# The inputs of a state-space convolution in a two-block kernel: four of its matmuls with whole fp32 weights

## The chip, the cores and the metric

The kernel runs on one core of a Trainium2 chip. A core has five engines, each with its own instruction order: TensorE (PE in the profile; its weight loads are shown apart as PEld), VectorE (DVE), ScalarE (ACT), GpSimd (POOL) and SyncE (SP), from which most transfers (DMAs) are issued. The metric is the device time of one execution in microseconds (us); lower is better.

## The reference

Two blocks run one after the other on 256 tokens of width 1024. The first is two layers of pooling, sparse attention and a feed-forward part. The second, which the change concerns, is a block with a state-space branch (SSD), a dilated attention branch and a feed-forward part, all in fp32. Cut to what matters here:

```python
def second_block(x, w_in, ...):
    u = h @ w_in
    z, xbc, dt_f_raw, dt_b_raw, q, k, v, gate_logits = jnp.split(u, ...)
    y_ssd = ssd_branch(z, xbc, dt_f_raw, dt_b_raw, conv_w, conv_b, ...) @ w_proj_ssd
    y_att = attention_branch(q, k, v) @ w_proj_attn
    gates = jax.nn.sigmoid(gate_logits + b_gate).reshape(bsz, s, N_BRANCHES, D_MODEL)
    mix = (gates[:, :, 0] * y_ssd + gates[:, :, 1] * y_att) @ w_out
    ...

def ssd_branch(z, xbc, ...):
    xbc = jax.nn.silu(centred_depthwise_conv(xbc, conv_w, conv_b))     # 5 taps
    xs, bm, cm = jnp.split(xbc, [D_INNER, D_INNER + SSD_GROUPS * D_STATE], axis=-1)
    ...
    y = (y_f + y_b + d_skip[:, None] * xh).reshape(...) * jax.nn.silu(z)
    # then a norm over each of the 4 groups
```

`w_in` has 1024 rows. The product `h @ w_in` is made in pieces of 512 columns; of `xbc` these are x0, x1, x2, x3 (the 2048 columns of `xs`, one piece for each of the 4 groups), B and C.

## The kernel before

*Weights.* All weights stream from HBM in chunks of 128 x 1024 fp32 (512 KB). `Weights.load` (line 129) issues a chunk's DMA on SP into a tile `wst` (5 buffers), and splits it in two: ScalarE copies it to `wh` in the type fp32r (line 140), VectorE subtracts this from `wst` and writes the rest, `wl` (line 141). `wh` and `wl` have 9 buffers each. Chunks are loaded in the order of the products, three ahead in block 2, at most four at once. `W.next()` hands out the next chunk.

*Products.* The activations are split in the same way, `hh` and `hl`. A product is three matmuls into the same PSUM bank: rest by whole, whole by rest, whole by whole. All matmuls are written by the helper `mm` (line 89), so all have line 89 in the profile and are told apart by their tiles. There are three forms. `Gemm.fm` makes the result with the channels on partitions: for each k of 128 rows and each of four column blocks, the weights are the stationary 128x128 block and 256 tokens stream (x0 to x3, B, C); records are `acc<-hh,wl 128x256`, `acc<-hl,wh`, `acc<-hh,wh`. `Gemm.tm` makes it with the tokens on partitions (q, k, v, z), streaming 512 weight columns: `acc<-wh,hl 128x512` and so on.

*Order.* In block 2 the products follow the list `order2`: v0 qk0 qk1 qk2 v1 B C x0 x1 z0 x2 z1 x3 z2 z3 g2 g3 pa g0 g1 ps. Each piece has four chunks (`x`: two k each, eight products of 128x256 a chunk). Between the products the other work of the block is issued, by generators that advance with each k: dilated attention beside B, C, x0 and x1; the state-space work of group g once xg and zg are there. The order of the instructions within each engine follows from it at build time by the scheduler of the language; on the chip each engine works its own list in that order and waits at its head.

*What follows an x.* `conv(name, c0)` (line 1316) evacuates the PSUM banks of x: ScalarE applies the middle tap and the bias (`cv<-acc,par`, line 1327), VectorE adds the other four taps (line 1330, four for each of four channel blocks, 16 in all), ScalarE makes a tanh (`page<-cv`, line 1331) and VectorE the product (line 1332). From the pages of B and C TensorE makes two products for each group (`tr<-page`, 128x256), which VectorE takes up as `cbu`, `cbl`, `cbo` (lines 1396 to 1398), and from an x page transposes (`tr<-cst,page`), which VectorE takes up as `xo` (line 1410). All of them write the one PSUM bank `tr`. ScalarE and VectorE further build decay matrices `R` and `G` (lines 1431 to 1446), with which TensorE makes `pv<-xt,R`.

*Where the activations come from.* At the end of layer 1, `done1(t)` calls `to_fm` for each half t of the tokens: TensorE transposes the residual into PSUM, ScalarE copies it to `hh` and VectorE subtracts to `hl`.

Of the kernel before, what the change touches and what calls it, by code (L numbers as in the profile page):

```python
# [17 lines left out]
S = 256  # L18
# [43 lines left out]
def tile_two_blocks(ctx: ExitStack, tc: tile.TileContext, I, out, stop=None, dbg=None):  # L62
# [59 lines left out]
    class Weights:  # L122


        def __init__(self):
            self.specs, self.ready, self.extra, self.rate, self.due = deque(), deque(), deque(), 0.0, 0.0
            self.live, self.used, self.depth, self.cap = 0, False, 0, NW

        def load(self, srcs, kc, n):
            st = wp.tile([128, SZ], FT, name="wst", bufs=NST)  # L130
            sv = st[:, :kc * n].rearrange("p (k n) -> p k n", k=kc)
            at = 0
            for src in srcs:
                w = src.shape[-1]
                nc.sync.dma_start(sv[:, :, at:at + w], src)
                at += w
            assert at == n
            h = wp.tile([128, SZ], FR, name="wh", tag="wh", bufs=NW)
            l = wp.tile([128, SZ], FR, name="wl", tag="wl", bufs=NW)
            A.activation(h[:, :kc * n], st[:, :kc * n], AF.Copy)  # L140
            V.tensor_tensor(l[:, :kc * n], st[:, :kc * n], h[:, :kc * n], op=OP.subtract)  # L141
            self.ready.append((h[:, :kc * n].rearrange("p (k n) -> p k n", k=kc),
                               l[:, :kc * n].rearrange("p (k n) -> p k n", k=kc)))
            self.due += self.rate
            while self.due >= 1.0 and self.extra:
                self.due -= 1.0
                self.step()
# [50 lines left out]
    class Gemm:  # L198


        def __init__(self, w, cols):
            self.n = sum(b - a for a, b in cols)
            self.K = w.shape[1]
            self.kc = min(self.K, SZ // self.n)
            for k0 in range(0, self.K, self.kc):
                kn = min(self.kc, self.K - k0)
                W.specs.append(([w[:, k0:k0 + kn, a:b] for a, b in cols], kn, self.n))

        def chunks(self):
            return [(k0, min(self.kc, self.K - k0)) for k0 in range(0, self.K, self.kc)]  # L210
# [19 lines left out]
        def fm(self, act, evac, tag="acc"):  # L230

            nct = self.n // 128
            banks = [bank(tag) for _ in range((nct + 1) // 2)]
            for k0, kn in self.chunks():
                h, l = W.next()
                for k in range(kn):
                    ah, al = act(k0 + k)
                    for c in range(nct):
                        o = banks[c // 2][:, (c % 2) * 256:(c % 2) * 256 + 256]
                        wh, wl = h[:, k, c * 128:(c + 1) * 128], l[:, k, c * 128:(c + 1) * 128]  # L240
                        mm(o, wl, ah, k0 + k == 0 and c % 2 == 0)
                        mm(o, wh, al, False)
                        mm(o, wh, ah, False, k0 + k == self.K - 1)
                    tick()
                    yield
            for b, p in enumerate(banks):
                evac(b, p)
# [204 lines left out]
    def new_h():  # L452
        return (xp.tile([128, 8, S], FR, name="hh", bufs=1), xp.tile([128, 8, S], FR, name="hl", bufs=1))

    def to_fm(t, xn, hi, lo, sc=None, sh=None):

        for kb in range(2):
            b = bank(("tr", "pv")[kb])
            for k in range(4):
                T.transpose(b[:, k * 128:(k + 1) * 128], xn[kb][:, k * 128:(k + 1) * 128], ident)  # L460
            src = b.rearrange("p (a b) -> p a b", a=4)
            if sc is not None:
                hf = t2([128, 4, 128], "hf")
                for k in range(4):
                    kk = kb * 4 + k
                    if kb:
                        A.activation(hf[:, k], src[:, k], AF.Identity, bias=sh[:, kk:kk + 1], scale=sc[:, kk:kk + 1])
                    else:
                        V.tensor_scalar(hf[:, k], src[:, k], sc[:, kk:kk + 1], sh[:, kk:kk + 1], op0=OP.mult, op1=OP.add)
                src = hf  # L470
            ks, tsl = slice(kb * 4, kb * 4 + 4), slice(t * 128, t * 128 + 128)
            split(hi[:, ks, tsl], lo[:, ks, tsl], src, A)


    lay = []
# [17 lines left out]
    for n in ORDER2 + ["o"]:  # L493
# [4 lines left out]
        elif n == "pa":  # L498
            g2[n] = Gemm(kt_view(I["w_proj_attn_2"]), [(0, D)])
        elif n == "ps":  # L500
            g2[n] = Gemm(kt_view(I["w_proj_ssd_2"]), [(0, D)])
        elif n == "o":
            g2[n] = Gemm(kt_view(I["w_out_2"]), [(0, D)])
        else:
            c = X0 + CONV2[n] * 128 if n in CONV2 else {"q": Q0, "z": Z0, "g": G0}[n[0]] + int(n[-1]) * 512
            g2[n] = Gemm(wi, [(c, c + 512)])
    ff2 = FeedForward(I["w_up_2"], I["w_down_2"])


# [609 lines left out]
    xn0 = [rms(t) for t in range(2)]  # L1119
    W.rate = TU["r0"]  # L1120
    W.extra.extend(mod_part(*m, TU["modp"]) for m in MODS["mix", 0])
    h1, h2_ = [], []

    def between0(c):
        if c == 4:
# [16 lines left out]
    def done1(t):  # L1142
        if not h2_:
            h2_.extend(new_h())
        to_fm(t, [xs[t][:, :512], xs[t][:, 512:]], *h2_)

    hybrid_layer(1, h1, None, done1)
    if stop == "l1":
# [167 lines left out]
    def conv(name, c0):  # L1316
# [14 lines left out]
            A.activation(fl(th), fl(cv), AF.Tanh, scale=0.5)  # L1331
            V.scalar_tensor_tensor(fl(th), fl(th), 1.0, fl(cv), op0=OP.add, op1=OP.mult)

        yield from g2[name].fm(aF, ev)
        cvo[name] = o[0]
        plan.got.add(name)

# [423 lines left out]
```

## Time and profile before

| | |
|---|---|
| time, three runs | 1280.6, 1282.55, 1288.57 us (median 1282.55) |
| profiled execution | 1284.53 us, of it 1282.4 us span |
| mean granted clock of TensorE | 0.967 |
| busy: TensorE, weight load | 1179.8 us (92%), 1037.6 us (81%) |
| busy: VectorE, ScalarE, GpSimd | 895.9 us (70%), 642.4 us (50%), 237.0 us (18%) |
| HBM read | 246.03 MB, 193 GB/s over the span |

The busy times are of the whole span. Times in the rows below count from the span's start. Block 2 begins at about 703 us; x0 begins at 787.15, x1 at 809.22, z0 at 825.97, x2 at 846.95, z1 at 861.67, x3 at 880.80, z2 at 896.98 and z3 at 921.33. A row of the timeline groups equal instructions that follow one another: its start, its length, the engine, the line, the operation, the tiles and their count. Matmuls overlap in the pipe, so that their cost is read from start to start. A wait is the time in which an engine had an instruction at its head that could not start, put down to the one that released it.

### The profile page before, as it was taken

Reading aid. Unit: us, or ns where it says so; the run is one execution under the profiler, and the core shown is the slowest. Engines: PE = TensorE matmul, PEld = TensorE weight load, DVE = VectorE, ACT = ScalarE, POOL = GpSimd, SP = SyncE. Lnnn points to the kernel's source line nnn. Section 1 sums busy time; section 2 is a strip of 40 time slices with the busy share of each in tenths; the row PEclk is TensorE's granted clock in tenths of the full one; section 3 lists DMA queues with packets and bytes.
Section 4 is the critical chain, followed back from the end, with each engine's and each line's share of the span. In section 5 each row is a group of like instructions: output and inputs, shape, how many; then the busy total and the mean of one; then the engine's idle time right before and its main releaser. Section 6 shows DMA issues by size and latency. Waiting matters only on the chain.

```text
span 1282.4 us, 19159 instructions
## 1 busy us (share of the span) xinstructions
PE 1179.8 (92%) x7188; PEld 1037.6 (81%) x7188; DVE 895.9 (70%) x1446; ACT 642.4 (50%) x1070; POOL 237.0 (18%) x233
## 2 busy tenths in 40 slices
PE   4878898999898899999999999988898899999997
PEld 3656776899787788789998999977688888799896
DVE  5777798887758768764545738799999557754544
ACT  4346355444535554744543545485675434544440
POOL 3553322112315101210100000011112001210101
PEclk9788889999999999999999999989899899999999
DMA  7855667889878534566663663564466753666640
GB/s 268 284 174 180 230 214 230 292 297 330 289 218 266 189 99 119 190 207 192 181 193 101 216 200 102 195 174 139 135 191 189 258 151 98 226 210 188 183 145 33
DMA packets 101780, 249.18 MB, mean 194 GB/s; under 512 B 9780, under 2 KB 15028, under 8 KB 101688
## 3 DMA queue, kind: packets, MB, share of 16 engines
q1 hardware_dynamic: 100904, 247.12, 60.6%
q8 instruction: 56, 0.92, 0.3%
q10 hardware_dynamic: 784, 0.85, 0.2%
q14 instruction: 36, 0.29, 0.1%
HBM read 246.03 MB, written 1.11 MB: 193 GB/s over the span
## 4 chain that ended last, share of the span: by engine, by line
PE 38%; issue 10%; DVE 8%; ACT 1%; POOL 1%; DMA 0%; DVEq 0%; POOLq 0%; ACTq 0%
PE acc L89 23%; PE st L89 12%; DVE wl L141 2%; DVE R L1444 1%; DVE cv L1330 1%; PE pv L89 1%; DVE G L1433 1%; DVE R L1446 1%; ACT wh L140 1%; POOL yss L119 0%; DVE ytmp L1465 0%; DMA wst<-in_w_up_dram 0%; PE tr L89 0%; POOL fr L380 0%; DVE yg L1477 0%
## 5 line engine op out<-in xcount | busy, mean ns | idle before, releaser
L141 DVE TENSOR_TENSOR wl<-wst,wh 128x1024 fp32r<-128x1024 f32 (+3 forms) x340 | 418.6, 1244 | 164.7 <-ACT wh L140 163.7
L140 ACT ACTIVATE wh<-wst 128x1024 fp32r<-128x1024 f32 (+3 forms) x340 | 352.1, 1048 | 314.2 <-PE acc L89 98.1
L89 PE MATMUL st<-hh,wh 128*128 128x256 f32 x576 | 163.0, 283 | 0.0
L89 PE MATMUL st<-hl,wh 128*128 128x256 f32 x576 | 163.0, 283 | 0.0
L89 PE MATMUL st<-hh,wl 128*128 128x256 f32 x576 | 163.0, 283 | 0.0
L89 PE MATMUL acc<-wh,frl 128*128 128x512 f32 x384 | 151.8, 395 | 2.4 <-DVE frl L381 2.3
L89 PE MATMUL acc<-wl,frh 128*128 128x512 f32 x384 | 150.6, 392 | 0.0
L89 PE MATMUL acc<-wh,frh 128*128 128x512 f32 x384 | 150.3, 391 | 0.0
L380 POOL TENSOR_TENSOR fr<-fr 128x512 f32<-128x512 f32 x48 | 64.7, 1349 | 384.7 <-ACT frh L379 376.4
L89 PE MATMUL acc<-hh,wl 128*128 128x256 f32 x416 | 122.1, 294 | 1.4 <-DVE wl L141 1.4
L89 PE MATMUL acc<-hl,wh 128*128 128x256 f32 x416 | 119.0, 286 | 0.0
L89 PE MATMUL acc<-hh,wh 128*128 128x256 f32 x416 | 118.7, 285 | 0.0
L89 PEld LDWEIGHTS st<-hh,wl 128*128 128x128 f32 x576 | 110.5, 192 | 0.7
L89 PEld LDWEIGHTS st<-hl,wh 128*128 128x128 f32 x576 | 110.5, 192 | 0.7
L89 PEld LDWEIGHTS st<-hh,wh 128*128 128x128 f32 x576 | 110.5, 192 | 0.0
L89 PE MATMUL acc<-wl,hh 128*128 128x512 f32 (+3 forms) x224 | 90.6, 405 | 13.1 <-DVE wl L141 13.1
L89 PE MATMUL acc<-wh,hl 128*128 128x512 f32 (+3 forms) x224 | 90.2, 413 | 12.4 <-ACT wh L140 9.9
L548 DVE SCALAR_TENSOR_TENSOR macc<-wst,cact,macc 128x1024 f32<-128x1024 f32 x70 | 91.7, 1311 | 7.5 <-DMA wst<-in_w_mod_dram 3.9
L89 PE MATMUL acc<-wh,hh 128*128 128x512 f32 (+3 forms) x224 | 90.6, 405 | 0.0
L89 PEld LDWEIGHTS acc<-wh,frl 128*128 128x128 f32 x384 | 72.6, 189 | 19.6 <-DVE frl L381 5.4
L89 PEld LDWEIGHTS acc<-wh,frh 128*128 128x128 f32 x384 | 72.5, 189 | 15.5
L89 PEld LDWEIGHTS acc<-wl,frh 128*128 128x128 f32 x384 | 72.5, 189 | 14.0
(328 smaller groups left out, 2289.6 us busy)
## 6 DMA issues: line engine op xcount, KB each, us to landing
wst<-in_w_ff_dram SPq DMA_DIRECT2D x128, 512.0 KB, 4.4
wst<-in_w_mod_dram SPq DMA_DIRECT2D x96, 512.0 KB, 4.6
wst<-in_w_in_dram SPq DMA_DIRECT2D x92, 512.0 KB, 4.8
wst<-in_w_up_dram SPq DMA_DIRECT2D x32, 512.0 KB, 4.3
wst<-in_w_down_dram SPq DMA_DIRECT2D x32, 512.0 KB, 4.3
wst<-in_w_out_dram SPq DMA_DIRECT2D x24, 512.0 KB, 4.2
R<-rows SPq DMA_DIRECT2D x32, 256.0 KB, 5.4
wst<-in_w_proj_ssd_dram SPq DMA_DIRECT2D x16, 512.0 KB, 4.7
```

What stands on the lines that cost most here:

```text
L89: T.matmul(o, l, r, start=start, stop=stop, skip_group_check=True)
L140: A.activation(h[:, :kc * n], st[:, :kc * n], AF.Copy)
L141: V.tensor_tensor(l[:, :kc * n], st[:, :kc * n], h[:, :kc * n], op=OP.subtract)
L380: G.tensor_tensor(r, r, r, op=OP.mult)
L548: V.scalar_tensor_tensor(acc, st, cact[:, k:k + 1], acc, op0=OP.mult, op1=OP.add)
L1330: V.scalar_tensor_tensor(v[:, a:e], u[:, a + j - 2:e + j - 2], w[:, j:j + 1], v[:, a:e], op0=OP.mult, op1=OP.add)
L1433: V.scalar_tensor_tensor(gm[:, i], cl, dt_[:, t, 32 + a0 + i:33 + a0 + i], gm[:, i], op0=OP.mult, op1=OP.add)
L1444: V.scalar_tensor_tensor(E[:, i], E[:, i], sums[:, t, h:h + 1], u[:, i], op0=OP.subtract, op1=OP.min)
L1446: V.tensor_tensor(E, E, ssd.pop(("G", g, t, sub)), op=OP.mult)
```

## The change

The four pieces x0 to x3 are loaded whole. Their chunks go by DMA straight into a buffer of the tag `wh` under the name `ww`; for them there is no `wst`, no `wh` copy on ScalarE and no `wl` on VectorE (16 chunks, so 16 fewer of each). A new `Gemm.fm_whole` multiplies each 128x128 block once, in fp32, with the unsplit activations `hw`. These are two tiles of 128 x 4 x 256, which `to_fm` fills in layer 1's end with one more ScalarE copy of 128x512 for each of its four transposed blocks. B, C and all others are as before.

```diff
-        def load(self, srcs, kc, n):
-            st = wp.tile([128, SZ], FT, name="wst", bufs=NST)
+        def load(self, srcs, kc, n, whole=False):
+            st = wp.tile([128, SZ], FT, name="ww", tag="wh", bufs=NW) if whole else wp.tile([128, SZ], FT, name="wst", bufs=NST)
...
             assert at == n
+            if whole:
+                self.ready.append((sv, None))
+                return
             h = wp.tile([128, SZ], FR, name="wh", tag="wh", bufs=NW)
...
-        def __init__(self, w, cols):
+        def __init__(self, w, cols, whole=False):
...
-                W.specs.append(([w[:, k0:k0 + kn, a:b] for a, b in cols], kn, self.n))
+                W.specs.append(([w[:, k0:k0 + kn, a:b] for a, b in cols], kn, self.n, whole))
...
+        def fm_whole(self, act, evac):
+
+            nct = self.n // 128
+            banks = [bank("acc") for _ in range((nct + 1) // 2)]
+            for k0, kn in self.chunks():
+                w, _ = W.next()
+                for k in range(kn):
+                    for c in range(nct):
+                        mm(banks[c // 2][:, (c % 2) * 256:(c % 2) * 256 + 256], w[:, k, c * 128:(c + 1) * 128], act(k0 + k),
+                           k0 + k == 0 and c % 2 == 0, k0 + k == self.K - 1)
+                    tick()
+                    yield
             for b, p in enumerate(banks):
...
-    def to_fm(t, xn, hi, lo, sc=None, sh=None):
+    def to_fm(t, xn, hi, lo, sc=None, sh=None, whole=None):
...
             split(hi[:, ks, tsl], lo[:, ks, tsl], src, A)
+            if whole:
+                A.activation(whole[kb][:, :, tsl], src, AF.Copy)
...
-            g2[n] = Gemm(wi, [(c, c + 512)])
+            g2[n] = Gemm(wi, [(c, c + 512)], n[0] == "x")
...
             h2_.extend(new_h())
-        to_fm(t, [xs[t][:, :512], xs[t][:, 512:]], *h2_)
+            hw.extend(t4([128, 4, S], "hw") for _ in range(2))
+        to_fm(t, [xs[t][:, :512], xs[t][:, 512:]], *h2_, whole=hw)
...
-        yield from g2[name].fm(aF, ev)
+        if name[0] == "x":
+            yield from g2[name].fm_whole(lambda k: hw[k // 4][:, k % 4], ev)
+        else:
+            yield from g2[name].fm(aF, ev)
```

The change also moves instructions within the engines' orders, as the scheduler places them anew at build time. Three places follow; line numbers of the changed kernel are some 20 higher.

TensorE at the end of x1 and the start of z0, before: x1's last pass is the `acc<-hh,wh` of 128x256, then z0's passes of 512 columns begin; `tr<-page` is a product of the pages of B and C, `tr<-cst,ya` belongs to the dilated attention.

```order
L89 MATMUL acc<-hh,wh 128x256
L89 MATMUL acc<-wh,hl 128x512
L89 MATMUL acc<-wl,hh 128x512
L89 MATMUL tr<-page 128x256
L89 MATMUL acc<-wh,hh 128x512
...
L89 MATMUL acc<-wh,hl 128x512
L1310 MATMUL tr<-cst,ya 128x128 x2
L89 MATMUL acc<-wl,hh 128x512
```

The same place in the changed kernel; `acc<-hw,ww` are x1's fp32 matmuls, `pv<-vp,dilT` the dilated attention.

```order
L89 MATMUL tr<-page 128x256
L89 MATMUL acc<-hw,ww 128x256 x4
L89 MATMUL pv<-vp,dilT 128x64
L89 MATMUL tr<-page 128x256
L89 MATMUL pv<-vp,dilT 128x64 x3
L89 MATMUL acc<-hw,ww 128x256 x4
L1332 MATMUL tr<-cst,ya 128x128 x2
L89 MATMUL acc<-hw,ww 128x256 x3
L1432 MATMUL tr<-cst,page 128x128 x4
L89 MATMUL acc<-hw,ww 128x256
L89 MATMUL acc<-wh,hl 128x512
L89 MATMUL acc<-wl,hh 128x512
```

The second `tr<-page`, the `tr<-cst,ya` (ten passes of z0 stood ahead of it) and the first `tr<-cst,page` have moved from z0 into the end of x1.

TensorE at the end of x3 and the start of z2, before: the second `tr<-page` stands behind 19 passes of z2.

```order
L89 MATMUL tr<-page 128x256
...
L89 MATMUL acc<-hh,wh 128x256
L89 MATMUL acc<-wl,hh 128x512
L89 MATMUL acc<-wh,hh 128x512
...
L89 MATMUL pv<-xt,R 128x64 x4
...
L89 MATMUL acc<-wl,hh 128x512
L89 MATMUL tr<-page 128x256
L89 MATMUL acc<-wh,hh 128x512
```

The same place in the changed kernel.

```order
L89 MATMUL acc<-hw,ww 128x256 x16
L89 MATMUL tr<-page 128x256
L89 MATMUL pv<-xt,R 128x64 x4
L89 MATMUL acc<-hw,ww 128x256 x2
L89 MATMUL tr<-page 128x256
L89 MATMUL acc<-hw,ww 128x256 x2
L89 MATMUL acc<-wh,hl 128x512
```

Both `tr<-page` now stand ahead of x3's last two matmuls.

SP's queue where block 2's `dil` loads (the bias of the dilated attention) stand between the weights, before and then in the changed kernel.

```order
L1267 DMA dil<-in_dbias_dram 128x512 x2
L135 DMA wst<-in_w_in_dram 128x2x512 x3
L1267 DMA dil<-in_dbias_dram 128x512
L135 DMA wst<-in_w_in_dram 128x2x512
L1267 DMA dil<-in_dbias_dram 128x512 x2
```

```order
L136 DMA ww<-in_w_in_dram 128x2x512 x3
L1289 DMA dil<-in_dbias_dram 128x512 x2
L136 DMA wst<-in_w_in_dram 128x2x512
L1289 DMA dil<-in_dbias_dram 128x512 x3
L136 DMA ww<-in_w_in_dram 128x2x512 x3
```

The `ww` chunks stand in the same queue among the same loads, the `dil` loads partly ahead of them.

## Rows read from the trace of the kernel before

**Rows 1.** The page's first part: busy time, share of the span, instructions of each engine.

```profile
PE 1179.8 (92%) x7188; PEld 1037.6 (81%) x7188; DVE 895.9 (70%) x1446; ACT 642.4 (50%) x1070; POOL 237.0 (18%) x233
```

**Rows 2.** Windows: length, busy PE, PEld, DVE, ACT, POOL, granted clock, DMA share, GB/s.

```profile
787.00:826.00 39.00, 39.00 (x311) 37.26 (x310) 31.88 (x67) 19.79 (x35) 0.00 (x0) 1.00 0.44 142
826.00:921.00 95.00, 80.12 (x448) 67.00 (x447) 89.49 (x196) 65.07 (x142) 13.54 (x12) 0.89 0.53 158
921.00:990.00 69.00, 63.24 (x431) 56.78 (x430) 64.49 (x121) 47.84 (x100) 12.97 (x12) 0.97 0.65 186
```

**Rows 3.** Waits of TensorE from 787 to 990 us: us in total, times, longest.

```profile
PE acc L89 <- ACT wh L140: 9.9, 2, 5.8
PE pv L89 <- DVE R L1446: 6.8, 8, 2.7
PE acc L89 <- DVE wl L141: 3.5, 3, 2.0
```

**Rows 4.** Chain of waits, 826 to 847 us: start, us, piece of work.

```profile
826.60 0.43 PE tr L89 x2
...
832.75 2.74 DVE cv L1330 x7
...
840.79 0.96 ACT wh L140
...
841.79 1.22 PE acc L89 x2
```

**Rows 5.** Timeline of TensorE at the ends of x1 and x3 and in z2.

```profile
825.97 0.40 PE L89 MATMUL acc<-wh,hl 128*128 128x512 f32 x1
...
896.86 0.28 PE L89 MATMUL acc<-hh,wh 128*128 128x256 f32 x1
...
915.08 1.74 PE L89 MATMUL acc<-wh,hl 128*128 128x512 f32 x3 [5.83 <-ACT wh L140]
...
918.34 0.63 PE L89 MATMUL acc<-wl,hh 128*128 128x512 f32 x1
918.77 0.63 PE L89 MATMUL acc<-wh,hh 128*128 128x512 f32 x1
```

**Rows 6.** Timeline of VectorE behind the end of x3.

```profile
903.26 0.29 DVE L1396 SCALAR_TENSOR_TENSOR cbu<-tr,cst 128x128 f32<-128x128 f32 x1 [0.52 <-PE tr L89]
...
905.67 0.86 DVE L1330 SCALAR_TENSOR_TENSOR cv<-acc,par,cv 128x254 f32<-128x254 f32 x2
```

**Rows 7.** Timeline of TensorE in x1: an fp32 product between fp32r passes.

```profile
820.22 0.28 PE L89 MATMUL acc<-hh,wh 128*128 128x256 f32 x1
820.34 0.60 PE L89 MATMUL tr<-page 128*128 128x256 f32 x2
820.59 0.47 PE L89 MATMUL acc<-hh,wl 128*128 128x256 f32 x1
820.89 0.28 PE L89 MATMUL acc<-hl,wh 128*128 128x256 f32 x1
```

**Rows 8.** Timeline of TensorE in C: three short fp32 products.

```profile
774.48 1.19 PE L89 MATMUL st<-page 64*128 64x256 f32 x6
775.60 0.38 PE L89 MATMUL acc<-hh,wl 128*128 128x256 f32 x1
```

**Rows 9.** Timeline of TensorE in block 1: fp32 passes of 64 columns.

```profile
147.78 3.18 PE L89 MATMUL pv<-vS,pT 128*128 128x64 f32 x27
150.77 0.47 PE L89 MATMUL acc<-wh,mh 128*128 128x512 f32 x1
```

**Rows 10.** Windows of `wl` on VectorE: length, busy, clock, DMA share, GB/s.

```profile
826.00:921.00 95.00, 22.80 (x19) 0.89 0.53 158
```

**Rows 11.** Window of z2, columns as in rows 2.

```profile
897.00:921.00 24.00, 17.73 (x79) 13.67 (x78) 23.01 (x55) 14.96 (x31) 3.22 (x3) 0.79 0.43 127
```

**Rows 12.** Timeline of ScalarE at the start of block 2.

```profile
706.70 0.60 ACT L103 ACTIVATE hh<-pv 128x512 fp32r<-128x512 f32 x1
```

**Rows 13.** The page's DMA issues: KB each, median us to landing.

```profile
wst<-in_w_in_dram SPq DMA_DIRECT2D x92, 512.0 KB, 4.8
```

More of the change, by code (lines that the diff above doesn't have):

```diff
@@ L243, in fm @@
                         mm(o, wh, ah, False, k0 + k == self.K - 1)
+                    tick()
+                    yield
+            for b, p in enumerate(banks):
+                evac(b, p)
+        def fm_whole(self, act, evac):
[7 more added lines that the diff above has]
+                           k0 + k == 0 and c % 2 == 0, k0 + k == self.K - 1)
                     tick()
@@ L1121, in tile_two_blocks @@
     W.extra.extend(mod_part(*m, TU["modp"]) for m in MODS["mix", 0])
-    h1, h2_ = [], []
+    h1, h2_, hw = [], [], []
     def between0(c):
```

## The prediction

> **What bounds the kernel now.** I read the busy table first, then the stretch of the span that the change touches, then the waits in it. Over the whole span TensorE is busy 92%, VectorE 70%, ScalarE 50% [rows 1], so TensorE bounds on average; but the four products x0 to x3 lie between 787 and 897 us, and there the average misleads. The windows show two regimes [rows 2]. In 787 to 826 us (x0 and x1) TensorE is busy all 39.00 us at a granted clock of 1.00, and VectorE 31.88: whatever TensorE gets to do more there, the end pays. In 826 to 921 us (z0, x2, z1, x3, z2) TensorE is busy 80.12 of 95 us at a mean clock of 0.89, and VectorE 89.49 of 95: VectorE bounds there. In 921 to 990 us both are nearly full (63.24 and 64.49 of 69).
>
> The waits of TensorE from 787 to 990 us name what it lacks [rows 3]: 9.9 us in two waits for a split `wh` of ScalarE, 6.8 us in eight for `R` of VectorE, 3.5 us in three for a `wl` of VectorE. The longer of the two `wh` waits is 5.8 us, so the other is 4.1: they are the fourth weight chunk of z0 (841.79 us) and that of z2 (915.08 us). The split of that chunk stands in ScalarE's order behind `page<-cv`, the end of x1's or x3's convolution. The chain of waits for z0 shows the links [rows 4]: a product `tr<-page` on TensorE at 826.60, the convolution on VectorE at 832.75, the split at 840.79, TensorE again at 841.79. From x1's last matmul, which hands over at 825.97 [rows 5], that is 15.8 us; from x3's (896.86) to 915.08 it is 18.2 us.
>
> Why does the convolution of x3 begin only at 905.67 us when its product was done at 897? In VectorE's rows the work before it stops at 903.26 with an idle 0.52 us for TensorE [rows 6]: the `cbu` that waits there stands in VectorE's order ahead of the convolution, and the product it reads (`tr<-page`) stood in TensorE's order behind 19 passes of z2. The same gate is at z0: the second `tr<-page` behind z0's second pass, the `tr<-cst,ya` behind its tenth.
>
> **The change, part by part.**
>
> *The matmul itself.* Each x is 32 products of a 128x128 block of weights with 256 columns. Removed: three fp32r passes for each of the 4 x 32; added: one fp32 matmul each, two records in the trace. Passes of 256 columns start 0.12 us apart (820.22, 820.34), so a product costs 0.36 now. The nearest fp32 row of the same shape is `tr<-page`: from 820.34 to 820.89 its two records and one pass of 0.12 fit, so it costs 0.43 [rows 7]. (The pass at 820.59 seems nearer, but lasts longer than its like; the next start is the clean one.) The upper end is `st<-page`, 512 fp32 columns in three short products, 774.48 to 775.60, 1.12 us, or 0.56 for 256 columns [rows 8]; the lower end is no loss, 0.36. I take 0.43, since the shape is the same and since the weight load should hide: 27 fp32 passes of 64 columns took 147.78 to 150.77, 0.11 each with their loads [rows 9], half of the 0.215 that a pass of 256 columns has. So +0.07 x 32 = 2.2 us for each x, +4.5 for x0 and x1 (0 to 12.8), +4.5 for x2 and x3.
>
> The Trainium skill, page "FP8 and Floating Point Precision", section "TensorE Precision Notes", says that true fp32 takes four passes through the array; with the 0.12 of a pass that would be 0.48 a product and +15.4 us in all, and speaks against the change. The 0.43 of the rows above lies between three and four such passes.
>
> *x0 and x1, 787 to 826 us.* TensorE is full, nothing covers: **+4.5**. What goes there on VectorE and ScalarE (eight `wl`, eight `wh`) buys nothing by itself.
>
> *VectorE, 826 to 921 us.* Nineteen `wl` took 22.80 us [rows 10], 1.20 each; the eight of x2 and x3 go, -9.6: VectorE's work falls from 89.5 to 79.9. TensorE's rises to 84.6, less what the half clock gives back. After the long wait, 512-column passes started 0.43 us apart (918.34, 918.77) [rows 5] and the granted clock of 897 to 921 was 0.79 [rows 11]: the lower of the two levels, 1.2 GHz, for part of it, after the engine had stood still. With 0.89 over 95 us some 10 us of clock are missing; much of that falls on idle time, and I take 4 us given back if the two long waits go.
>
> *The gates move.* In the changed order both `tr<-page` and the `tr<-cst,ya` stand ahead of x1's last product, and both `tr<-page` ahead of x3's last two (rows of TensorE's order, above). So VectorE is no longer held by z0's and z2's passes before it may begin the convolution; of the 6.8 us from 825.97 to 832.75 and the 8.8 from 896.86 to 905.67, most can go, as far as VectorE has no older work, and the 9.6 us taken from it say that it has less. The first three chunks of z0 and z2 give TensorE about 12 us (the 15.8 less the wait of 4.1; 18.2 less 5.8): a split that comes 12 us after x's end is in time. Taken: z0's wait -4, z2's -5, the small ones for `wl` and `R` -2, the clock -4, x2 and x3 +4.5: **-10.5**. The stretch becomes 84.5 us with 79.9 of VectorE, 95% busy, as it is now (94%); it cannot fall much further.
>
> *921 to 990 us.* None of its weights is touched; a VectorE that comes in less late is worth **-1** (0 to -4).
>
> *ScalarE's four new copies* (`hw`, 128x512, 0.60 us each as the `hh` copy at 706.70 [rows 12]) stand at the end of layer 1, where the first product of block 2 already runs with the first half; 2.4 us behind it: **0**, +1 if that cover is gone.
>
> *SP's queue.* A whole chunk waits for a slot of `wh`, which TensorE frees, where before it waited for a `wst` that VectorE freed; `dil` and `R<-rows` loads stand behind it. A chunk lands 4.8 us after its issue [rows 13] and is asked for three chunks ahead, 3 x 8 x 0.43 = 10 us: covered, **0**; without that cover up to 4.8 for each x.
>
> **Sum.** Against the profiled run, 1284.5 us (span 1282.4): +4.5 - 10.5 - 1 = 1277.5. The median of the runs shown is 1282.55, 2 us under the profiled one, so I expect **1276 us**; its own range is 1270 to 1281.
>
> **The rivals.**
> All waits go. If VectorE comes early enough everywhere, the 20.2 us of the three largest waits and some 6 us of half clock go against +9 of TensorE: -17, 1265 us. For it: the gates all moved forward. Against: VectorE would have to be 100% busy in what is left. Chance 0.15.
> *Slower:* the latency stays. If the split of z0's fourth chunk still comes 15 us or more after x1's last product and z2's 18 (since the chain from `tr<-page` through `R`, convolution and `page` is other work than the removed `wl`, of which none stands in it), the two waits remain, TensorE's +9 is paid in full, and only 2 us of small waits go: +7, 1290 us. For it: no `wl` is in the chain of rows 4. Against: the moved gates. It decides from a latency of 15 us on. Chance 0.15.
> *No change:* a new wait takes the gain: TensorE waits for a whole chunk directly (4.8 us once or twice, the load stuck in SP's queue behind a slot or behind `R<-rows`), or only one of the two long waits goes: 1282 us. Chance 0.15.
> *The product is dearer.* At four passes of 0.12, 0.48 a product, the sum grows by 0.05 x 128 = 6.4 to 1282; at 0.56 by 16.6, of which the slack left in 826 to 921 us swallows little: 1290. Chance 0.10. The four passes of the page named above are this case.
>
> **How the numbers follow.** The forecast has 0.45, the rivals 0.15, 0.15, 0.15 and 0.10. The range 1266 to 1288 leaves out the far half of the first rival, most of the slower one and the dearest product, about 0.2. A change of 1% (12.8 us) is about what a measurement of this kernel can tell from none: faster than 1269.7 us is the first rival and the forecast's lower tail, 0.18; slower than 1295.4 needs the latency to stay and the product to be dear, 0.06; the rest 0.76.
>
> **What would show it.** Right: passes `acc<-hw,ww` start 0.21 to 0.22 us apart, 0.43 a product; x0 and x1 together last about 43.5 us; the first convolution op of x1 starts under 4 us after x1's last product; the waits of TensorE for `wh` fall from 9.9 to under 2 us; VectorE is busy about 80 us from x1's end to z2's fourth chunk, some 10 us shorter; the granted clock there is nearer 1. Wrong: a start-to-start above 0.24; a wait for `ww<-in_w_in_dram`; the two `wh` waits still there; or a new pause at the end of layer 1.

## The result and the profile after

The changed kernel takes 1269.5 us (median of four runs, 1264.5 to 1270.9) where the kernel before took 1281.6 beside it (1278.5 to 1288.6): a ratio of 0.9891, 95% interval 0.9842 to 0.9940. That is 12 us, 1.1%, faster. The forecast was 1276 us with a range of 1266 to 1288. The measured time lies in the range, but 0.5 us below the likeliest case's own range (1270 to 1281), just inside the tail "faster than 1269.7" that had 0.18, and nearer to the rival "all waits go" (1265) than to the forecast. So the direction and the place were right, and a size was not.

The profiled execution has a span of 1267.9 us against 1282.4. The busy table answers to [rows 1]:

```profile
PE 1179.0 (93%) x7060; PEld 1033.1 (81%) x7060; DVE 879.4 (69%) x1430; ACT 628.7 (50%) x1058; POOL 233.5 (18%) x233
```

TensorE's busy time is the same (1179.8 before): its dearer products and what the faster clock gives back about cancel in it (worked out below). The windows of the same three stretches answer to [rows 2] (length, busy time of TensorE, weight load, VectorE, ScalarE and GpSimd, granted clock, DMA share, GB/s):

```profile
787.00:826.00 39.00, 39.00 (x224) 34.00 (x222) 25.51 (x62) 14.51 (x28) 0.00 (x0) 1.00 0.28 85
826.00:921.00 95.00, 93.01 (x456) 76.21 (x455) 90.31 (x208) 67.85 (x156) 15.04 (x14) 1.00 0.59 180
921.00:990.00 69.00, 63.87 (x485) 60.37 (x484) 64.26 (x109) 45.81 (x90) 12.05 (x10) 0.98 0.67 212
```

In 826 to 921 us TensorE is now busy 93.01 us where it was 80.12, at a granted clock of 1.00 where it was 0.89. VectorE is as full as before (90.31, before 89.49): it has not become idle, it does more of the work in the same time. The waits of TensorE from 787 to 990 us answer to [rows 3]:

```profile
PE pv L89 <- DVE R L1471: 4.7, 4, 2.6
PE acc L89 <- ACT sig L1384: 1.3, 2, 0.9
PE acc L89 <- DVE wl L145: 0.5, 1, 0.5
PE tr L89 <- DVE cbo L1423: 0.4, 1, 0.4
PE acc L89 <- ACT wh L144: 0.2, 1, 0.2
```

The two long waits for `wh` (9.9 us) are 0.2 us, those for `wl` 0.5 where they were 3.5, and there is none for `ww`.

**Where the time went, by pieces.** Starts of the pieces are read from the timeline of TensorE. The length of block 1 varies by up to 4.4 us from execution to execution (the first product of block 2 starts at 699.3 to 703.7 us in the profiles below, and x0 at 783 to 788 us, but for the one kernel in which B and C ahead of it are dearer), so I measure from the start of x0 to the start of g2, which spans x0, x1, z0, x2, z1, x3, z2 and z3, and from there to the end of the span.

| kernel | x0 starts | g2 starts | x0 to g2 | g2 to end |
|---|---|---|---|---|
| before | 787.15 | 936.66 | 149.5 | 345.7 |
| changed | 785.33 | 922.93 | 137.6 | 345.0 |

The 11.9 us that the stretch is shorter are the gain that the runs show (12 us). The two spans differ by 14.5 us: 1.8 lie ahead of x0, in block 1, and 0.7 behind g2's start, no more than such stretches vary. TensorE stood still 15.2 us in the stretch before (waits of 4.1, 5.8 and six smaller ones) and 2.0 now, 13.2 less. The other 1.3 us go the other way: its work is 134.3 us before (149.5 - 15.2) and 135.6 now, although the products cost 9 us more. The remaining 7.7 us came back, mostly with the clock: in the kernel before, passes of 512 columns started 0.43 us apart behind the waits [rows 5], now they start 0.23 apart, and 21 such passes at 843 to 846, 877 to 880 and 918 to 921 us make 4 of the 7.7. The rest was not taken apart.

9.6 us of the 11.9 are won up to z2's fourth chunk (915.08 - 787.15 = 127.9 us before, 903.67 - 785.33 = 118.3 now), 2.3 behind it.

The price of the product is as forecast. The timeline of TensorE in x2:

```profile
845.76 2.32 PE L89 MATMUL acc<-hw,ww 128*128 128x256 f32 x10
847.92 1.00 PE L89 MATMUL pv<-xt,R 128*128 128x64 f32 x8
```

Ten records take 845.76 to 847.92, 0.216 us each, two to a product: 0.43, with their weight loads hidden.

The relief of VectorE shows at the convolution of x3, which began at 905.67 us, 8.7 us after x3's last product [rows 5, 6]. The work of VectorE ahead of it (`R`, `G`, two `wl`, `yg`, `cbu`) is the same string in both kernels. It began here before, 108.0 us after x0's start:

```profile
895.19 2.16 DVE L1444 SCALAR_TENSOR_TENSOR R<-R,sums 128x128 f32<-128x128 f32 x4
```

and in the changed kernel here, 98.8 us after x0's start, with the convolution behind it:

```profile
884.12 2.15 DVE L1469 SCALAR_TENSOR_TENSOR R<-R,sums 128x128 f32<-128x128 f32 x4
894.81 3.21 DVE L1352 SCALAR_TENSOR_TENSOR cv<-acc,par,cv 128x254 f32<-128x254 f32 x8
```

x3's product hands over to z2 in the meantime:

```profile
893.52 0.58 PE L89 MATMUL acc<-wh,hl 128*128 128x512 f32 x1
```

VectorE comes to the string 9.2 us earlier, which is about the 9.6 us of the eight subtractions of x2 and x3, and the convolution begins 1.3 us after x3's last product.

At x1 the picture is another one. x1's last records on TensorE:

```profile
829.54 0.60 PE L89 MATMUL acc<-hw,ww 128*128 128x256 f32 x2
```

and VectorE behind them:

```profile
825.31 0.29 DVE L1421 SCALAR_TENSOR_TENSOR cbu<-tr,cst 128x128 f32<-128x128 f32 x1
828.57 0.42 DVE L106 TENSOR_TENSOR yal<-tr,yah 128x256 fp32r<-128x256 f32 x1
831.69 3.20 DVE L1352 SCALAR_TENSOR_TENSOR cv<-acc,par,cv 128x254 f32<-128x254 f32 x8
```

`cbu` and `yal` wait for nothing, and the convolution begins at 831.69, 1.9 us after x1's product hands over to z0 (829.79), where it was 6.8 [rows 4, 5]. But counted from x0's start it begins at 46.4 us, where it began at 45.5: it is not earlier. x1's product ends later, 44.5 us after x0's start where it was 38.8, since x0 and x1 are 4.5 us dearer and since products that stood in z0 moved into x1 (1.1 us). So z0's wait was filled by TensorE's own work, and not removed by a faster VectorE. Part of the string ahead of this convolution begins with a load in both kernels, here before and then in the changed one:

```profile
825.78 1.28 ACT L1443 ACTIVATE R<-R,sums 128x128 f32<-128x128 f32 x4 [7.27 <-DMA R<-rows]
```

```profile
825.81 1.28 ACT L1468 ACTIVATE R<-R,sums 128x128 f32<-128x128 f32 x4 [3.23 <-DMA R<-rows]
```

No run here moves that load alone, so what sets the start of x1's convolution stays open.

Of the other signs of the prediction: the convolution of x1 starts under 4 us after its product, as expected, but for the reason above; x0 and x1 last 44.5 us together (43.5 expected); from x1's end to z2's fourth chunk VectorE is busy 70.4 of 73.9 us where it was 83.6 of 89.1 (about 80, some 10 us shorter, was expected).

### The profile page after: what moved, and what is told of

It reads as the page before. It is cut to its first block, busy times and chain, and to the rows that moved or that the text cites. A ratio compares the mean times of both kernels' runs of the same rounds, so it can differ in the third digit from the quotient of the medians.

```text
span 1267.9 us, 18858 instructions
## 1 busy us (share of the span) xinstructions
PE 1179.0 (93%) x7060; PEld 1033.1 (81%) x7060; DVE 879.4 (69%) x1430; ACT 628.7 (50%) x1058; POOL 233.5 (18%) x233
## 4 chain that ended last, share of the span: by engine, by line
PE 41%; issue 9%; DVE 5%; DMA 2%; ACT 1%; POOL 1%; DVEq 0%; POOLq 0%; ACTq 0%
PE acc L89 26%; PE st L89 12%; DVE wl L145 2%; PE pv L89 1%; DMA wst<-in_w_down_dram 1%; PE tr L89 1%; DVE R L1469 1%; DMA wst<-in_w_in_dram 1%; DVE G L1458 0%; ACT wh L144 0%; DMA R<-rows 0%; DVE R L1471 0%; POOL yss L119 0%; POOL fr L399 0%; ACT G L1456 0%
## 5 line engine op out<-in xcount | busy, mean ns | idle before, releaser
L145 DVE TENSOR_TENSOR wl<-wst,wh 128x1024 fp32r<-128x1024 f32 (+3 forms) x324 | 401.1, 1250 | 164.3 <-ACT wh L144 163.0
L144 ACT ACTIVATE wh<-wst 128x1024 fp32r<-128x1024 f32 (+3 forms) x324 | 335.8, 1048 | 310.4 <-PE acc L89 107.0
L89 PE MATMUL acc<-wl,hh 128*128 128x512 f32 (+3 forms) x224 | 89.1, 398 | 11.6 <-DVE wl L145 11.6
L89 PE MATMUL acc<-wh,hh 128*128 128x512 f32 (+3 forms) x224 | 88.0, 393 | 0.0
L89 PE MATMUL acc<-hh,wl 128*128 128x256 f32 x288 | 83.3, 289 | 0.0
L89 PE MATMUL acc<-hl,wh 128*128 128x256 f32 x288 | 83.0, 288 | 0.0
L89 PE MATMUL acc<-hh,wh 128*128 128x256 f32 x288 | 82.1, 285 | 0.0
```

What stands on the lines that cost most here:

```text
L89: T.matmul(o, l, r, start=start, stop=stop, skip_group_check=True)
```

## Experiments: what the gain is made of

Two theories. **A**: VectorE bounds z0 to z2, and the gain is the subtractions taken off it. **G**: the gain is that the gates (`tr<-page`, `tr<-cst,ya`) moved forward in TensorE's order. Beside them stands the question where the dearer product is paid. Ratios are to runs of the kernel before on the same chip in the same session (its median there was 1283.5 to 1283.9 us), from six or twelve runs of each kernel; the column x0 to g2 is of one profiled execution each.

| kernel | ratio, 95% interval | median us | x0 to g2 | g2 to end |
|---|---|---|---|---|
| changed, again | 0.9894 (0.9868 to 0.9920) | 1269.9 | 138.0 | 345.1 |
| e1 gates early, all split | 1.0008 (0.9985 to 1.0031) | 1283.9 | 147.4 | 347.9 |
| e2 changed, gates late | 0.9931 (0.9907 to 0.9954) | 1273.9 | 140.5 | 347.1 |
| e3 changed, VectorE's work kept | 1.0004 (0.9980 to 1.0029) | 1283.2 | 150.6 | 347.4 |
| e11 changed, ScalarE's work kept | 0.9934 (0.9909 to 0.9959) | 1274.9 | 138.5 | 345.9 |
| e9 split, subtractions left out | 0.9911 (0.9882 to 0.9941) | 1272.0 | 138.1 | 349.5 |
| e4 x2, x3 whole | 0.9916 (0.9884 to 0.9948) | 1272.5 | 139.4 | 349.7 |
| e5 x0, x1 whole | 1.0009 (0.9991 to 1.0027) | 1286.0 | 150.4 | 347.5 |
| e8 x1, x2, x3 whole | 0.9886 (0.9855 to 0.9917) | 1268.9 | 135.7 | 344.2 |
| e7 B, C and x0 to x3 whole | 0.9951 (0.9930 to 0.9972) | 1276.9 | 138.2 | 349.5 |
| e10 x1, x2, x3, g2, g3 whole | 0.9879 (0.9847 to 0.9911) | 1267.3 | 135.7 | 341.0 |
| e6 subtractions on GpSimd | 1.0021 (1.0005 to 1.0038) | 1285.6 | 151.4 | 350.4 |

The waits shown below are those of TensorE from 780 to 990 us (us in total, times, longest), the windows have the columns of [rows 2]. The last column, mostly the same work in all, runs from 341 to 350 us: a single profile tells differences of the whole span only to some 3 us, which is why the stretch is shown apart.

### The changed kernel again

> The changed kernel itself, unchanged, timed beside the next three on the same chip: 0.989 of the kernel before, as on record, whichever theory holds. It is the measure for the differences of 2 to 5 us between the next ones.

Measured 0.9894, and 138.0 us from x0 to g2: the stretch repeats within 0.4 us in these two executions. Differences of 1 us in the column x0 to g2 can be read, if with care.

### e1: the gates alone

```diff
-TU = dict(... d0=50, ... scb=5, ...)
+TU = dict(... d0=49, ... scb=8, ...)
```

> The kernel before, all weights split, only the planner's numbers changed (scb 5 to 8, d0 50 to 49), so that in TensorE's order both tr<-page stand in x1 (18 or more passes ahead of its end), the tr<-cst,ya behind three passes of z0 instead of ten, and the second tr<-page of x3 behind four passes of z2 instead of nineteen. VectorE's work is unchanged. Theory G (the gain comes from the gates that moved): the two long waits for wh (9.9 us) fall under 3 us and the time is 8 us or more under the kernel before, about 1273 us. Theory A (it comes from the eight subtractions taken off VectorE in z0 to z2): VectorE stays 94% busy there, at most 2 us are won, about 1280 us.

No gain (1.0008). The waits of TensorE, and the window, of this kernel:

```profile
PE acc L89 <- ACT wh L140: 8.7, 2, 4.8
PE pv L89 <- DVE R L1446: 5.5, 6, 2.6
PE acc L89 <- DVE wl L141: 5.1, 3, 2.5
```

```profile
826.00:921.00 95.00, 80.88 (x448) 68.31 (x447) 89.19 (x191) 64.25 (x134) 13.42 (x13) 0.91 0.53 156
```

The two `wh` waits are 8.7 us where they were 9.9, the wait for `wl` rose by 1.6, and VectorE is busy 89.19 us of 95. With the gates moved VectorE still has older work to do before it comes to the convolution of x3, which begins 6.9 us after x3's last product (8.7 before, 1.3 in the changed kernel). 2.1 us of the stretch were won, and they are not seen in the time. Theory G falls as the main cause.

### e2: the gates late, the weights whole

```diff
-TU = dict(... d0=50, ... scb=5, ...)     # of the changed kernel
+TU = dict(... d0=51, ... scb=3, ...)
```

> The changed kernel with the planner's numbers set later (scb 5 to 3, d0 50 to 51): in TensorE's order tr<-cst,ya stands behind ten passes of z0 as in the kernel before, and the second tr<-page behind 29 passes of z2 instead of ahead of x3's end. Theory G: the waits for wh come back, 4 us in z0 and 6 us in z2, with the half clock behind them, about 1280 us. Theory A: VectorE has the room, the time stays within 3 us of the changed kernel, about 1271 us.

The gain stays for the most part: 0.9931, 140.5 us. The wait for `wh`:

```profile
PE acc L89 <- ACT wh L144: 0.5, 1, 0.5
```

In the trace the second `tr<-page` of x3 stands behind 35 passes of z2 (29 of them behind the first), and still the convolution of x3 begins 1.2 us after x3's last product. This is no clean test of the gate, though: VectorE's order moved too, and the `cbu` that reads this product now stands behind the convolution:

```profile
895.27 0.47 DVE L1352 SCALAR_TENSOR_TENSOR cv<-acc,par,cv 128x254 f32<-128x254 f32 x1
...
906.59 0.28 DVE L1421 SCALAR_TENSOR_TENSOR cbu<-tr,cst 128x128 f32<-128x128 f32 x1
```

What it shows is that early products on TensorE are not needed for most of the gain. The stretch is 2.5 to 2.9 us longer than the changed kernel's, about what e1 won with early gates; the time, 4 us longer by the medians, is a little more than the 3 us that were expected, with intervals that overlap.

### e3: VectorE's work kept

```diff
             if whole:
                 self.ready.append((sv, None))
+                l = wp.tile([128, SZ], FR, name="wl", tag="wl", bufs=NW)
+                V.tensor_tensor(l[:, :kc * n], st[:, :kc * n], st[:, :kc * n], op=OP.subtract)
                 return
```

> The changed kernel with a subtraction of 128x1024 on VectorE for each of the 16 whole chunks, into a wl tile that nothing reads: VectorE's work as before, ScalarE's copies still gone. Theory A: the 9.6 us that VectorE was relieved of in z0 to z2 are back while TensorE keeps its +9 us, so the time is at or over that of the kernel before, 1281 to 1290 us. Theory G: TensorE's order has the gates early here too, so most of the gain stays, 1271 to 1274 us.

The gain is gone: 1.0004 and 150.6 us, although ScalarE's copies are gone and the gates stand early at x1 (at x3 the second `tr<-page` is behind 23 passes of z2, where it was behind 19).

```profile
PE acc L89 <- ACT wh L146: 7.6, 2, 6.6
PE pv L89 <- DVE R L1473: 6.4, 9, 2.6
```

```profile
826.00:921.00 95.00, 83.88 (x396) 67.60 (x395) 89.12 (x192) 58.28 (x134) 13.54 (x12) 0.95 0.55 161
```

The wait of z2's fourth chunk is back, 6.6 us, and the clock is 0.95 where it was 1.00. VectorE's string ahead of x3's convolution begins 109.7 us after x0's start (108.0 before, 98.8 in the changed kernel), and the convolution 11.1 us after x3's last product. TensorE waits for no `ww`, so a longer hold on its buffer did not reach TensorE. Sixteen subtractions that nothing reads cost the gain. Theory A holds.

### e11: ScalarE's work kept

```diff
+                h = wp.tile([128, SZ], FR, name="wl", tag="wl", bufs=NW)
+                A.activation(h[:, :kc * n], st[:, :kc * n], AF.Copy)
                 return
```

> The changed kernel with a ScalarE copy of 128x1024 for each of the 16 whole chunks, into a wl tile that nothing reads: ScalarE's work as before, VectorE's subtractions gone. The counterpart of the kernel that kept VectorE's. Theory A: ScalarE is at most 71% busy from 826 to 921 us (67.9 of 95) and its copies are not the limit, so the time stays within 2 us of the changed kernel, 0.988 to 0.991 of the kernel before. Rival (the copies of x2 and x3 held up the page and the split of z2's fourth chunk behind it, in ScalarE's order): a wait for wh of 3 us returns at z2, 0.992 or more.

The stretch is 138.5 us, 0.5 to 0.9 over the changed kernel, and no wait for `wh` returns:

```profile
PE acc L89 <- ACT wh L146: 0.6, 1, 0.6
```

```profile
826.00:921.00 95.00, 92.20 (x453) 75.78 (x452) 90.39 (x207) 71.47 (x154) 15.03 (x14) 1.00 0.60 181
```

The rival's wait did not come. The ratio, 0.9934, is above what was expected (0.988 to 0.991) and would fit the rival's (0.992 or more); its interval overlaps that of the changed kernel. By the medians ScalarE's copies are worth 5 us, which the intervals do not tell from none, and the stretch speaks for 1.

### e9: the subtractions left out, three passes kept

```diff
-            l = wp.tile([128, SZ], FR, name="wl", tag="wl", bufs=NW)
+            l = h if nosub else wp.tile([128, SZ], FR, name="wl", tag="wl", bufs=NW)
             A.activation(h[:, :kc * n], st[:, :kc * n], AF.Copy)
-            V.tensor_tensor(l[:, :kc * n], ...)
+            if not nosub:
+                V.tensor_tensor(l[:, :kc * n], ...)
...
-            g2[n] = Gemm(wi, [(c, c + 512)])
+            g2[n] = Gemm(wi, [(c, c + 512)], n[0] == "x")
```

> The kernel before with the subtractions for x0 to x3 left out: the three passes use wh where wl stood, so that part of the computation (the rest of these weights) is replaced. TensorE, ScalarE and the transfers have the same work as before; VectorE is relieved as by the change. Theory A: VectorE's relief is the gain, and without the dearer product it is 5 to 9 us larger than the changed kernel's: 1261 to 1266 us; the wh waits fall under 2 us. Rival (the gain needs the whole chunks, one wait less in the chain of the load, or ScalarE's relief): 1275 us or more.

This is the run that tells most. The kernel leaves out the rest of these weights, so it makes only part of the computation and is read for its time alone. The relief of VectorE brings the gain, 0.9911 and 138.1 us, as the change does, with the split, the copies and the three passes kept. (The gates moved forward here too, the second `tr<-page` of x3 from behind 19 passes of z2 to behind 8; e1 shows that this alone brings nothing.) VectorE's string ahead of x3's convolution begins 98.1 us after x0's start. But TensorE has 9 us less to do here than in the changed kernel, and that brings nothing more: I expected 1261 to 1266 us. The waits and the window:

```profile
PE acc L89 <- ACT wh L140: 6.0, 2, 3.1
PE pv L89 <- DVE R L1447: 5.3, 7, 2.5
```

```profile
826.00:921.00 95.00, 87.65 (x496) 73.80 (x495) 90.09 (x203) 72.57 (x157) 14.93 (x14) 0.95 0.58 175
```

TensorE comes to the fourth chunks of z0 and z2 sooner, and waits there, 6.0 us, part of the time at the lower clock; VectorE is as full as ever. So behind x1 VectorE sets the time with fp32r as with fp32, and the dearer products of x2 and x3 fill time that TensorE would have stood still. The account does not close to the last us: e8 below, with x0 split and 6.7 us more for TensorE than here, has a stretch 2.4 us shorter than e9. ScalarE's copies (1 us by e11) and the waits with their lower clock stand here and not there; which of them it is was not separated.

### e4, e5 and e8: which of the four pieces

```diff
-            g2[n] = Gemm(wi, [(c, c + 512)], n[0] == "x")
+            g2[n] = Gemm(wi, [(c, c + 512)], n in ("x2", "x3"))          # e4
+            g2[n] = Gemm(wi, [(c, c + 512)], n in ("x0", "x1"))          # e5
+            g2[n] = Gemm(wi, [(c, c + 512)], n in ("x1", "x2", "x3"))    # e8
...                                                                      # the same test in conv
```

> Only x2 and x3 whole; x0 and x1 split as before. By the sum of the prediction x0 and x1 save their +4.5 us (TensorE is full there), but in TensorE's order the gates at the end of x1 stand as before (second tr<-page and tr<-cst,ya in z0), so z0's wait of 4 us and its half clock stay: about equal to the changed kernel, 1268 to 1271 us. If the gates at x1 do not matter (theory A: x2's and x3's subtractions are what counts): 1265 us.

> Only x0 and x1 whole; x2 and x3 split as before. Theory A (VectorE's relief within z0 to z2 is what counts, and this kernel's relief lies in 787 to 826 us, where VectorE had room): +4.5 us of TensorE are paid, z0's wait of 4 us goes since the gates at x1 move, z2's wait stays: about as before, 1281 to 1284 us. If relief ahead of 826 us counts as much as behind it: 1276 us.

> x1, x2 and x3 whole, x0 split. By the stage rule (a dearer product is paid in full where TensorE is full, and VectorE's relief ahead of x1 buys nothing) it saves the 2.2 us of x0 and keeps the rest: 2 us under the changed kernel, 1268 to 1270 where that has 1270 to 1272. Rival: x0's subtractions, which end at 797 us, hold VectorE up until x1's convolution: no better than the changed kernel, or 1 to 2 us slower.

x2 and x3 alone (e4) bring most of it, 0.9916 and 139.4 us, and keep z0's wait of 4.1:

```profile
PE acc L89 <- ACT wh L144: 4.1, 1, 4.1
```

x0 and x1 alone (e5) bring nothing, 1.0009; z0's wait goes, z2's stays, and those for `wl` too:

```profile
PE acc L89 <- ACT wh L144: 6.0, 2, 5.8
PE acc L89 <- DVE wl L145: 4.9, 4, 2.9
```

Leaving x0 split and x1 to x3 whole (e8) takes 135.7 us, 1.9 to 2.3 less than all four: by the stretch x0's +2.2 is paid in full, as the stage rule says, and its relief buys nothing. Splitting x1 too (e4) adds 3.7 us: x1's whole product costs 2.2 more on TensorE, but saves z0's wait and its half clock. By the stretch, then, the border between paying and not paying lies between x0 and x1; the times (e4 1272.5, all four 1269.9, e8 1268.9 us) have the same order, but their intervals overlap.

### e7: B and C whole as well

```diff
-            g2[n] = Gemm(wi, [(c, c + 512)], n[0] == "x")
+            g2[n] = Gemm(wi, [(c, c + 512)], n in CONV2)
...                                                                      # the same test in conv
```

> The changed kernel with B and C whole as well. In 703 to 787 us TensorE is busy all the time and VectorE 58%: by the stage rule the dearer product is paid in full and buys nothing, +4.5 us over the changed kernel, 1274 to 1275 us, and B and C last 2.2 us longer each. If VectorE's relief carries forward into z0 to z2: no worse than the changed kernel, 1269 to 1271 us.

0.9951 and 1276.9 us, 7 over the changed kernel where 4.5 were expected; from B's start to x0's the profile has 33.3 us, the changed kernel 28.7, +4.6. The stretch x0 to g2 is unchanged (138.2). Its window ahead of x0:

```profile
703.00:787.00 84.00, 84.00 (x543) 78.31 (x541) 35.93 (x71) 27.89 (x45) 0.00 (x0) 1.00 0.68 209
```

TensorE full, VectorE 43%: there the dearer product is paid whole and buys nothing. Of the 7 us, 2.4 are not explained by this; they are no more than the last column varies.

### e10: the two gates that VectorE still holds up

```diff
-            g2[n] = Gemm(wi, [(c, c + 512)], n[0] == "x")
+            g2[n] = Gemm(wi, [(c, c + 512)], n in ("x1", "x2", "x3", "g2", "g3"))
...                                                                      # the same test in conv
-        return g2[f"g{i}"].fm(aF, ev)
+        return g2[f"g{i}"].fm_whole(lambda k: hw[k // 4][:, k % 4], ev) if i > 1 else g2[f"g{i}"].fm(aF, ev)
```

> x1, x2, x3 and also g2 and g3 whole (x0 split). In 921 to 990 us of the changed kernel both engines are nearly full (TensorE 64.0, VectorE 64.1 of 69), and TensorE still waits 4.7 us for R of VectorE. If VectorE sets that stretch: -3 us against x1 to x3 alone, 1266 us; if TensorE does: +4.5 less the waits, 1269 to 1272 us. I expect the second.

1267.3 us, 0.9879, the lowest of all medians, if not apart from e8 (0.9886) or from the changed kernel (0.9894) by their intervals. In its profile the wait for `R` is down from 4.7 us to

```profile
PE pv L89 <- DVE R L1471: 0.8, 1, 0.8
```

```profile
921.00:990.00 69.00, 66.76 (x441) 61.04 (x439) 54.72 (x100) 43.10 (x86) 9.12 (x9) 1.00 0.68 216
```

and from x0 to the start of ps it has 207.2 us, e8 210.6, the changed kernel 213.0, the kernel before 225.3. I had expected TensorE to set that stretch (1269 to 1272 us); by the profile VectorE did.

### e6: the subtractions on GpSimd

```diff
-            V.tensor_tensor(l[:, :kc * n], st[:, :kc * n], h[:, :kc * n], op=OP.subtract)
+            (G if pool else V).tensor_tensor(l[:, :kc * n], st[:, :kc * n], h[:, :kc * n], op=OP.subtract)
...
-            g2[n] = Gemm(wi, [(c, c + 512)])
+            g2[n] = Gemm(wi, [(c, c + 512)], n[0] == "x")
```

> The kernel before with x0 to x3 split as ever and multiplied in three passes, but their 16 subtractions on GpSimd in place of VectorE. It relieves VectorE as the change does, without the +9 us of TensorE. Theory A: a gain at least that of the changed kernel, 1262 to 1270 us, if GpSimd (3.2 us busy of 24 in z2) makes a subtraction of 128x1024 in under 3 us, in time for the next chunk. Rival: GpSimd is so slow that TensorE waits for wl, 1285 us or more.

1.0021: nothing won, a little lost, and not for the rival's reason. GpSimd made each in 2.4 us (median), and TensorE waited only 0.9 us for `wl`; it waited for `R` of VectorE (and 5.5 us for `wh`):

```profile
PE pv L89 <- DVE R L1446: 14.6, 10, 4.1
```

GpSimd in x2, and VectorE at the same time:

```profile
842.25 7.27 POOL L141 TENSOR_TENSOR wl<-wst,wh 128x1024 fp32r<-128x1024 f32 x3 [8.19 <-ACT wh L140]
```

```profile
842.42 2.47 DVE L1433 SCALAR_TENSOR_TENSOR G<-cbl,dt__6387,G 128x128 f32<-128x128 f32 x1
844.82 5.39 DVE L1444 SCALAR_TENSOR_TENSOR R<-R,sums 128x128 f32<-128x128 f32 x4
```

One `G` took 2.47 us and four `R` 5.39; in the kernel before four of either take 1.14:

```profile
846.58 1.14 DVE L1444 SCALAR_TENSOR_TENSOR R<-R,sums 128x128 f32<-128x128 f32 x4
847.63 1.14 DVE L1433 SCALAR_TENSOR_TENSOR G<-cbl,dt__6387,G 128x128 f32<-128x128 f32 x4
```

VectorE stood inside its instructions while GpSimd worked, and was busy 89.49 us of the 95, as before. Its string ahead of x3's convolution begins 110.2 us after x0's start, 108.0 before. The relief did not take place.

## Why the prediction was right in its direction and short in its size

**What bounds.** Right. TensorE's full stretch ahead of x1 pays (e7, and e8 by its stretch), VectorE bounds behind it (e3, e9). What is shown of VectorE is shown at z2's wait; z0's wait is another matter (two paragraphs down).

**The price of the product.** Right: 0.43, 9 us in all. As for the page "FP8 and Floating Point Precision" of the Trainium skill, section "TensorE Precision Notes", with its four passes: if each record is two passes, one takes 0.108 us, so the trace can be read as four passes; what was too dear was to price them at the 0.12 of an fp32r pass. The rival at 0.48 falls.

**x0 and x1: +4.5, "nothing covers".** Half right. x0's 2.2 is paid (e8). x1's is covered by z0's wait, as e4 (x1 split, the wait of 4.1 stays) and e5 (x1 whole, it goes) show; the sum counted it in full and then took off z0's wait, which gives nearly the same (from x0's start to z0's fourth chunk: 54.6 us before, 55.5 after; +0.5 in the sum). But the sum gave z0's wait to the gates and the relief, and there luck helped: the convolution of x1 is no earlier, and the dearer product itself filled the wait.

**VectorE, -10.5 in z0 to z2, then -1.** Right mechanism, mis-sized. In the sum the waits gave 11 us (4, 5, 2) and the clock 4, against +9: -6. Measured from x0 to g2: waits 13.2, clock and small moves 7.7, against +9: -11.9. Most of the miss, 3.7 us, is the term for the clock, with the small moves that were not told apart from it. I had said that 10 us of clock were missing and put more than half of it on idle time; the granted clock of the stretch is 1.00 now, and most of it came back. The other 2.2 us are waits: 15.2 stood there, of which the sum took 11, and only 2.0 are left; the small ones for `wl` and `R` between z0 and z2 alone were 4.8, counted as 2.

**"It cannot fall much further": VectorE 95% busy.** The share was right, the amount was not. From x1's end to z2's fourth chunk VectorE is busy 83.6 of 89.1 us before and 70.4 of 73.9 now, 95% as forecast. But its work there fell by 13.1 us and not by the 9.6 of eight subtractions, because x1 ends 5.6 us later (counted from x0's start) and more of VectorE's older work is done by then: from x0's start to x1's end it is busy 30.0 us where it was 31.9, though eight subtractions went there too. So the floor was reckoned with too much work in it. Counted from x0's start, z2's fourth chunk begins 9.6 us earlier, as much as the eight subtractions took; the sum had -6 up to there.

**The gates.** The step that failed as a reason. [rows 6] had its price in it: of the 8.7 us ahead of x3's convolution VectorE stood 0.52 us for `tr`, and from 826 to 921 us this, with the 2.41 us at x1's end, is nearly all that it lost to the gates (waits of VectorE, us in total, times, longest):

```profile
DVE cbu L1396 <- PE tr L89: 3.2, 3, 2.4
```

Nearly all the rest of the 8.7 us was older work of VectorE, which the prediction names ("as far as VectorE has no older work") and did not count out. The gates moved as the order shows, but are worth 2 to 3 us of the stretch (e1, e2). Without VectorE's relief the time shows nothing of them (e1); with it the long waits go even with late products on TensorE (e2), though there VectorE's order had moved as well.

**The rivals.** "The latency stays" rested on the chain of [rows 4] having no `wl` in it. True, and beside the point at x3: the chain begins where VectorE takes its older work up, and that was late. "A new wait" did not come: no wait for `ww`, which lands 4.8 us after its issue (median) as `wst` did. The copies `hw` left no pause in the first product of block 2: v0 lasts 10.3 us before and after.

What stays open: how the gain of e10 beyond e8 stands in the time, since their intervals overlap; whether ScalarE's copies are worth 1 us (the stretch) or more (the ratio of e11); what holds e9's stretch 2.4 us over e8's; and what the load of `R<-rows` ahead of x1's convolution is worth, which no run moves by itself.

## To carry to other kernels

Where a second engine bounds a stretch, price an edit by what it takes off that engine, and count the dearer work on the waiting engine as covered up to its waits; then look for the border at which the engines change places, piece by piece, since the same edit pays on one side and costs on the other (x0, B and C here). Look at the clock beside the waits: here 13.2 us of waits went, the granted clock of the stretch z0 to z2 rose from 0.89 to 1.00, and more came back than the waits. Where an engine comes late to an instruction, count how much of the delay is idle time and how much is older work, before an order is blamed (0.52 of 8.7 us here). A helper engine is only a relief if the bounding engine's instructions keep their length beside it: read their durations, not only the helper's.

## What the runs showed of the hardware

GpSimd's subtraction of two SBUF tiles (128x1024, 2.4 us each) held VectorE's instructions up for its length: a `G` of 128x128 took 2.47 us (e6) where four take 1.14 in the kernel before. The convolution's `cv`, whose first input is in PSUM, stayed at 0.47 us on average. The Trainium skill says it in "SBUF — State Buffer", section "SBUF: two separate sides": VectorE instructions with two SBUF inputs and GpSimd share a pair of ports, held by one of them for a whole instruction. The trace agrees, and e6's expectation should have named it.
